# A hybrid layer whose weights come packed by quarters, and half of x transposed: x's second half scaled by VectorE alone, and other steps for heads and gate rows

## The chip, the cores and the metric

The kernel runs on one core of one Trainium2 chip. The metric is device microseconds from start to end of one execution, median over runs. The kernel before took 1518.96 us (three runs: 1516.54, 1518.96, 1522.65).

## What is computed

One layer of a hybrid encoder for one sequence of 1024 tokens of width 2048, all in float32:

```
h = RMSNorm(x) * norm_w
proj = h @ w_in                      # 2048 -> 6656 columns: rq rk rv rg | aq ak av ag
y_ret = groupnorm(retention(rq, rk, rv)) * silu(rg)      # 8 heads x 128, both directions, chunks of 128
y_att = window_attention(aq, ak, av, sink) * silu(ag)    # 8 heads, 2 kv heads, window of 128
out = RMSNorm(x + concat(y_ret, y_att) @ w_out) * final_norm_w
```

The two projections hold nearly all of the arithmetic.

## The kernel before

**Products.** A float32 matrix is split into a high and a low part of a matmul type. `mm3` multiplies high by high, high by low and low by high, so a product of two tiles is three matmuls (lines 99, 100 and 101). The high part is a cast by ScalarE (`wH`, line 88), the low part a subtraction by VectorE (`wL`, line 85).

**Blocks, products, steps.** The input projection is done in blocks of 512 columns by half of the 2048 rows of `w_in`, 26 of them in four phases. A block is not four quarter products but seven products of sums and differences (numbers 1, 2, 6, 5, 7, 3, 4). The sums on the weights' side are made while the kernel runs from the block's four quarters `a11`, `a12`, `a21`, `a22` (loaded by `quarter`) and a temporary `s2`; those of x's side (`c1` to `c7`) are made once for each half of x's columns. A product is four steps of two PSUM banks by three matmuls, so 24 matmuls of 128x512; a block is 28 steps. `pj` are the banks: two (`X`) for products 1, 6, 7 and 4, two (`Y`) for 2, 5 and 3. `evict` takes a finished bank away into a tile `ct`: ScalarE copies after products 1, 6, 5 and 4, VectorE adds after the others.

**What sets the order.** TensorE, SyncE (which issues most DMAs) and GpSimd run in the order in which the program is written; for VectorE and ScalarE a scheduler picks the order at build time, except in a few pinned places. At run time every engine works its own list strictly in order. `advance()` stands after every step of a product; it is the kernel's clock. All other work (turning x, rotary, the heads, attention, gates) is written as jobs, generators that are advanced once a step, so a `yield` in a job moves what follows by one step, and `idle(n)` by n. `prepare()` makes one product's operand a product ahead, in two buffers each of `wH` and `wL`, so a cast waits until the product two before has been multiplied.

**x.** x's first 1024 columns are transposed by TensorE at the start. Its second 1024 columns come in `second_part()` (line 489) while the blocks of the first phase run: 16 loads `xp` of 256 KB, 16 scalings by the row's `rms` on VectorE (line 500), 64 transposes on TensorE (line 463, in groups of four) and 16 copies by ScalarE that multiply by `norm_w` (line 464). The tile `src` that comes out feeds the sums for phases 2 and 4 (additions are line 92, subtractions line 95). `scale_first()` spreads `rms` along a row for the first half (`factors`, `rows`) and scales with it.

**Heads.** `head(h)` (line 824) runs eight times, one after the other: decays, scores (line 841), `vd`, v scaled by ScalarE (line 855, four operations), outer products of k and `vd` (line 870), states, results.

**Gates and the seam.** In the last phase `gating()` (line 1298) starts. `gate()` loads eight gate rows and eight rows of mixed heads, one pair after another, and `mix_in()` multiplies them into `ysrc` (line 1328). `puts()` makes the operand sums for the output projection from `ysrc` while the last block still runs, and the projection starts as they come. Its weights come as half quarters (line 1218).

Of the kernel before, what the change touches and what calls it, by code (L numbers as in the profile page):

```python
# [9 lines left out]
F32 = mybir.dt.float32  # L10
# [8 lines left out]
P = 128  # L19
# [19 lines left out]
M = 4  # L39
# [19 lines left out]
def hybrid_layer_kernel(  # L59
    ctx: ExitStack,  # L60
    tc: tile.TileContext,
    x, w_in, w_out, norm_w, decay_fwd, decay_bwd, gn_w, gn_b, sink, final_norm_w,
    rot_r, rot_a, dist_f, dist_b, steps, band,
    out,
):
    nc = tc.nc
    x, w_in, w_out, out = x[0], w_in[0], w_out[0], out[0]

# [39 lines left out]
    def blk(i, n=1):  # L108
        return slice(i * P, (i + n) * P)
# [19 lines left out]
    def idle(n):  # L129
        for _ in range(n):  # L130
            yield
# [49 lines left out]
    wp = ctx.enter_context(tc.tile_pool(name="wp", bufs=1))  # L181
    w_v = w_in.rearrange("(k p) c -> p k c", p=P)

# [11 lines left out]
    def quarter(part, b, n, k):  # L195
        t = wp.tile([P, M, 2 * P], F32, name=f"a{n}{k}", tag=f"a{n}{k}")
        k0, c0 = (2 * part + k - 1) * M, BLOCKS[b] + 2 * P * (n - 1)
        nc.sync.dma_start(out=t, in_=w_v[:, k0:k0 + M, c0:c0 + 2 * P])
        return t
# [259 lines left out]
    def turn(dst, parts, k):  # L459

        pt = ax()
        for i, part in enumerate(parts):
            nc.tensor.transpose(pt[:, blk(i)], part, ident)
        nc.scalar.activation(out=dst, in_=pt, func=AF.Copy, scale=nw[:, k:k + 1])
# [24 lines left out]
    def second_part():  # L489
        x2 = x[:, PART:].rearrange("s (h c) -> s h c", h=2)  # L490
        src = None
        for j in range(2):
            for m in range(2):
                xp = []
                for t in range(4 * m, 4 * m + 4):
                    xp.append(st.tile([P, 2, 2 * P], F32, name="xp", bufs=4))
                    nc.sync.dma_start(out=xp[-1], in_=x2[blk(t), :, 2 * P * j:2 * P * (j + 1)])
                yield from idle(10)
                for i in range(4):
                    nc.vector.tensor_scalar(out=xp[i], in0=xp[i], scalar1=rms[:, 4 * m + i:4 * m + i + 1], scalar2=None, op0=ALU.mult)  # L500
                yield from idle(3)
                if src is None:
                    src = st.tile([P, 2, M, S], F32, name="src", tag="src")
                for s in range(2):
                    for i in range(2):
                        turn(src[:, s, 2 * j + i, half(m)], [xp[t][:, s, blk(i)] for t in range(4)], (2 + s) * M + 2 * j + i)
                        yield
        parts_of(1, src)
        for sums, _ in parts[1]:
            yield from idle(4)  # L510
            sums()
# [6 lines left out]
    def half_of_a11(k0):  # L518
        c0 = BLOCKS[units[0][1]]
        nc.sync.dma_start(out=a11[:, k0:k0 + 2], in_=w_v[:, k0:k0 + 2, c0:c0 + 2 * P])  # L520

# [236 lines left out]
    def retention():  # L758
        with right("ret") as ret:
# [64 lines left out]
            def head(h):  # L824
# [7 lines left out]
                while h and turned.get(h - 1) != 2:  # L832
                    yield
                yield
                kT, qT = kq.pop(("kT", h)), kq.pop(("qT", h))
# [17 lines left out]
                for d in range(2):  # L853
                    for m in range(2):
                        nc.scalar.mul(vd[:, m * M:m * M + M, d].rearrange("p c (a j) -> p c a j", a=NB), v[m], kd[:, d * RH + h:d * RH + h + 1])
                    yield
                while h not in ks:
                    yield
# [204 lines left out]

    def scale_first():

        yield
        yield
        factors, rows = (st.tile([P, HALF], F32, name=n, tag="xp", bufs=4) for n in ("factors", "rows"))
        rows_of.append(rows)
        nc.vector.tensor_copy(out=chunks(factors), in_=rms[:, 0:4].rearrange("p (t o) -> p t o", o=1).broadcast_to([P, 4, P]))  # L1070
# [4 lines left out]
        nc.scalar.copy(out=rows, in_=pt)  # L1075
        yield

# [117 lines left out]
    free = set()  # L1195
    wo_v = w_out.rearrange("(k p) c -> p k c", p=P)
    wo_ = ctx.enter_context(ExitStack())
# [32 lines left out]
    def out_operands():  # L1230

        at = dict(PLACES)
        for u in range(len(OUT)):
# [16 lines left out]
            if u == len(OUT) - 1:  # L1250
                again = combp.tile([P, 2, 2, HALF], F32, name="again", tag="c1")
                part, pair = OUT[u]
                for j in range(2):
                    nc.sync.dma_start(out=again[:, j], in_=wo_v[:, M + 2 * j:M + 2 * j + 2, half(2 * pair + 1)])
                for j in range(2):
# [42 lines left out]
    def gating():  # L1298
# [13 lines left out]
        def operand_tiles(part, gates):  # L1312
# [18 lines left out]
            def gate():  # L1331
                asked = 0
                for i in range(2 * M):
# [229 lines left out]

_INS = ["x", "w_in", "w_out", "norm_w", "decay_fwd", "decay_bwd", "gn_w", "gn_b", "sink", "final_norm_w"]
_OUTS = [((1, S, D), "float32")]
# [24 lines left out]
```

## Time and profile before

| what | before |
|---|---|
| median of three runs | 1518.96 us |
| the profiled execution | 1518.94 us, its span 1517.2 us |
| TensorE busy | 1493.9 us, 98% |
| VectorE, ScalarE, GpSimd busy | 1111.8 us, 687.7 us, 150.0 us |
| moved by DMA | 318.91 MB, mean 210 GB/s |
| DMA packets under 2 KB | 110882 of 189704 |

Matmuls are pipelined: a 128x512 matmul is listed with some 0.39 us, but the next starts 0.23 us after it, so TensorE's pace is read from the starts. A window row of the profile gives for a stretch the busy time of each engine with its count of instructions, the clock that TensorE was granted (1.00 is full) and the DMA engines' busy share and GB/s. A wait row names the instruction that stood, what it waited for, the time in all, how often, and the longest.

### The profile page before, as it was taken

How to read it: one execution, taken by the hardware profiler on the slowest of the kernel's cores; microseconds unless marked ns; L12 is line 12 of the kernel's file. 1: busy time of each engine (PE TensorE's matmuls, PEld its weight loads, DVE VectorE, ACT ScalarE, POOL GpSimd, SP SyncE). 2: the span in 40 equal slices, each digit the busy share in tenths (PEclk: the TensorE clock that was granted, in tenths of full speed). 3: DMA queues.
4: the chain of work that ended last, by engine and by line, in shares of the span. 5: the costliest groups of instructions: out<-in, count | busy, mean ns of one | idle time of the engine just before them, and what ended most of it. 6: DMA issues, size and time to landing. Idle time of an engine off the chain costs nothing.

```text
span 1517.2 us, 20252 instructions
## 1 busy us (share of the span) xinstructions
PE 1493.9 (98%) x7214; PEld 1256.4 (83%) x7214; DVE 1111.8 (73%) x1935; ACT 687.7 (45%) x1123; POOL 150.0 (10%) x177
## 2 busy tenths in 40 slices
PE   9999999999999999999999999999999999999997
PEld 7888888788888888888888888887888788888886
DVE  6896594657758585867988989887656946776766
ACT  6553462234535453533534544444444563542425
POOL 0000001121010000001211100000211102020001
PEclk9999999999999999999999999999999999999999
DMA  8279847889675527798867765499896889495656
GB/s 319 70 269 327 312 167 182 221 212 253 160 221 194 199 93 224 266 332 188 164 178 177 190 201 168 146 318 318 216 262 163 185 194 209 88 209 171 212 179 252
DMA packets 189704, 318.91 MB, mean 210 GB/s; under 512 B 31618, under 2 KB 110882, under 8 KB 180771
## 3 DMA queue, kind: packets, MB, share of 16 engines
q1 hardware_dynamic: 165554, 266.74, 53.7%
q0 software_dynamic: 19728, 36.71, 16.3%
q10 hardware_dynamic: 4320, 14.17, 2.7%
q8 instruction: 57, 0.93, 0.3%
q14 instruction: 45, 0.36, 0.1%
HBM read 197.23 MB, written 128.71 MB: 215 GB/s over the span
## 4 chain that ended last, share of the span: by engine, by line
PE 72%; issue 10%; DVE 8%; DMA 6%; ACT 1%; SPq 1%; POOL 1%; ACTq 0%; POOLq 0%; DVEq 0%
PE pj L101 18%; PE pj L100 18%; PE pj L99 18%; PE ax L100 5%; PE ax L101 4%; PE ax L99 4%; DMA pr<-ct 2%; DVE wL L85 2%; PE ax L870 2%; DMA xt<-in_x_dram 1%; PE ax L653 1%; DVE ct L92 1%; DMA q<-pr 1%; PE ax L841 1%; PE ax L921 1%
## 5 line engine op out<-in xcount | busy, mean ns | idle before, releaser
L99 PE MATMUL pj<-c,wH 128*128 128x512 f32 x1444 | 574.3, 398 | 0.1
L101 PE MATMUL pj<-c,wL 128*128 128x512 f32 x1440 | 563.3, 391 | 2.3 <-DVE wL L85 2.2
L100 PE MATMUL pj<-c,wH 128*128 128x512 f32 x1444 | 563.6, 390 | 0.0
L101 PEld LDWEIGHTS pj<-c,wL 128*128 128x128 f32 x1440 | 270.7, 188 | 61.7 <-DVE wL L85 4.4
L99 PEld LDWEIGHTS pj<-c,wH 128*128 128x128 f32 x1444 | 271.7, 188 | 51.2 <-ACT wH L88 0.5
L100 PEld LDWEIGHTS pj<-c,wH 128*128 128x128 f32 x1444 | 272.0, 188 | 50.8 <-DVE c L999 0.2
L85 DVE TENSOR_TENSOR wL<-a,wH 128x1024 fp32r<-128x1024 f32 x157 | 191.5, 1220 | 116.6 <-ACT wH L88 109.6
L88 ACT CAST wH<-a 128x1024 fp32r<-128x1024 f32 (+1 forms) x159 | 166.2, 1045 | 227.2 <-PE pj L100 138.6
L325 ACT COPY ct<-pj 128x512 f32<-128x512 f32 x192 | 110.7, 584 | 183.6 <-PE pj L101 182.5
L92 DVE TENSOR_TENSOR ct<-pj,ct 128x512 f32<-128x512 f32 x164 | 109.3, 686 | 53.6 <-PE pj L101 50.1
L289 POOL DMA_DIRECT2D pr<-ct x88 | 78.0, 958 | 543.9 <-DVE ct L92 466.2
L85 DVE TENSOR_TENSOR wL<-s,wH 128x1024 fp32r<-128x1024 f32 x56 | 68.3, 1220 | 54.0 <-ACT wH L88 47.0
L100 PE MATMUL pj<-wL,c 128*128 128x512 f32 x224 | 88.2, 394 | 2.7 <-DVE wL L85 2.7
L99 PE MATMUL pj<-wH,c 128*128 128x512 f32 x224 | 87.8, 392 | 0.0
L101 PE MATMUL pj<-wH,c 128*128 128x512 f32 x224 | 87.8, 392 | 0.0
L100 PE MATMUL ax<-wL,c 128*128 128x512 f32 x208 | 81.2, 390 | 0.1
L101 PE MATMUL ax<-wH,c 128*128 128x512 f32 x208 | 81.0, 389 | 0.0
L99 PE MATMUL ax<-wH,c 128*128 128x512 f32 x208 | 81.0, 389 | 0.0
L88 ACT CAST wH<-s 128x1024 fp32r<-128x1024 f32 x56 | 58.9, 1052 | 37.8 <-DVE s L95 12.8
L100 PEld LDWEIGHTS pj<-wL,c 128*128 128x128 f32 x224 | 42.4, 189 | 12.2 <-DVE wL L85 3.6
L643 ACT ACTIVATE s<-s,nm 128x385 f32<-128x385 f32 (+1 forms) x64 | 37.6, 589 | 28.5 <-DVE nm L638 25.8
L947 ACT ACTIVATE y<-y,mv,rstd 128x128 f32<-128x128 f32 x64 | 26.9, 485 | 51.2 <-DVE mv L945 51.1
(242 smaller groups left out, 2053.2 us busy)
## 6 DMA issues: line engine op xcount, KB each, us to landing
a<-in_w_in_dram SPq DMA_DIRECT2D x103, 512.0 KB, 6.1
kept<-c SPq DMA_DIRECT2D x28, 1024.0 KB, 7.3
c<-kept SPq DMA_DIRECT2D x28, 1024.0 KB, 9.4
pr<-ct SPq DMA_DIRECT2D x94, 256.0 KB, 4.8
pr<-ct POOLq DMA_DIRECT2D x88, 256.0 KB, 6.0
a<-in_w_out_dram SPq DMA_DIRECT2D x18, 512.0 KB, 5.2
rx<-pr SPq DMA_DIRECT2D x64, 128.0 KB, 5.8
ysrc<-pr ACTq DMA_DIRECT2D x16, 512.0 KB, 5.1
```

The lines of the kernel that those rows point to most:

```text
L85: return nc.vector.tensor_tensor(out=dst, in0=src, in1=high.bitcast(F32), op=ALU.subtract)
L88: behind(pinned, nc.scalar.copy(out=dst_h, in_=src))
L92: nc.vector.tensor_tensor(out=dst, in0=a, in1=b, op=ALU.add)
L99: nc.tensor.matmul(po, aH, bH, start=first, stop=False, **kw)
L100: nc.tensor.matmul(po, aH, bL, start=False, stop=False, **kw)
L101: nc.tensor.matmul(po, aL, bH, start=False, stop=last, **kw)
L289: nc.gpsimd.dma_start(out=dst, in_=t, accum_op=ALU.add)
L325: nc.scalar.copy(out=t, in_=bank)
L643: nc.scalar.activation(out=s[:, 0:w + 1], in_=s[:, 0:w + 1], func=AF.Exp, scale=-1.0, bias=nm, accum_out=den)
L653: nc.tensor.transpose(pt[:, blk(j)], s[:, blk(j)], ident)
L870: nc.tensor.matmul(p, k_tok[:, c // 2, :, c % 2], vd[:, c, d], start=True, stop=True)
L947: nc.scalar.activation(out=y[:, c], in_=y[:, c], func=AF.Identity, scale=rs[:, c:c + 1], bias=mv[:, c, 0:1])
```

## The change

Three things are changed together.

1. `w_in` is given packed: each quarter of a block (128 partitions x 4 x 256) is one contiguous piece of 512 KB, so that a partition's part is 4 KB in one run where it was four runs of 1 KB. `w_out` is packed likewise, 4 KB in one run where it was two of 2 KB.
2. x's second 1024 columns are given transposed as `x_t`, in addition to x. `second_part()` now waits for step 66, loads four pieces of 1 MB at steps 66, 69, 72 and 75 straight into `src`, spreads `rms` of the second 512 tokens along rows (one VectorE copy, four transposes, one ScalarE copy) and scales `src` with eight operations of 128x1024 on VectorE, one a step from step 85. `factors` and `rows` get tiles of their own.
3. A head's scores come after two steps where it was one, its outer products after one more step. The waits between gate rows of the first part are 5 steps for the first four rows and 4 for the others, where all were 6.

By the program's own count of steps, the second part is ready at step 92 where it was 117. Heads' scores move from steps 435, 464, 488, 516, 540, 568, 592, 620 to 436, 465, 491, 518, 544, 571, 597, 624. The gating job starts at 651 where it was 646, but asks for its first row at 656 in both. Its eighth row of the first part is mixed at 710 where it was 718, and the sums of the output projection's products 2 and 6 are made at 713 and 717 where it was 718 and 720.

```diff
     def quarter(part, b, n, k):
         t = wp.tile([P, M, 2 * P], F32, name=f"a{n}{k}", tag=f"a{n}{k}")
         k0, c0 = (2 * part + k - 1) * M, BLOCKS[b] + 2 * P * (n - 1)
-        nc.sync.dma_start(out=t, in_=w_v[:, k0:k0 + M, c0:c0 + 2 * P])
+        nc.sync.dma_start(out=t, in_=w_in[k0 // M, c0 // (2 * P)])
         return t
...
     def second_part():
-        x2 = x[:, PART:].rearrange("s (h c) -> s h c", h=2)
-        src = None
-        for j in range(2):
-            for m in range(2):
-                xp = []
-                for t in range(4 * m, 4 * m + 4):
-                    xp.append(st.tile([P, 2, 2 * P], F32, name="xp", bufs=4))
-                    nc.sync.dma_start(out=xp[-1], in_=x2[blk(t), :, 2 * P * j:2 * P * (j + 1)])
-                yield from idle(10)
-                for i in range(4):
-                    nc.vector.tensor_scalar(out=xp[i], in0=xp[i], scalar1=rms[:, 4 * m + i:4 * m + i + 1], scalar2=None, op0=ALU.mult)
+        yield from idle(66 - clock[0])
+        src = st.tile([P, 2, M, S], F32, name="src", tag="src")
+        for s in range(2):
+            for j in range(2):
+                nc.sync.dma_start(out=src[:, s, 2 * j:2 * j + 2], in_=x_t[s][:, 2 * j:2 * j + 2])
                 yield from idle(3)
-                if src is None:
-                    src = st.tile([P, 2, M, S], F32, name="src", tag="src")
-                for s in range(2):
-                    for i in range(2):
-                        turn(src[:, s, 2 * j + i, half(m)], [xp[t][:, s, blk(i)] for t in range(4)], (2 + s) * M + 2 * j + i)
-                        yield
+        rows = rows_of[1]
+        yield from rows_from(rms[:, 4:8], rows[:, half(1)])
+        yield from idle(4)
+        for s in range(2):
+            for k in range(M):
+                i = (2 + s) * M + k
+                nc.vector.scalar_tensor_tensor(out=src[:, s, k], in0=src[:, s, k], scalar=nw[:, i:i + 1], in1=rows, op0=ALU.mult, op1=ALU.mult)
+                yield
         parts_of(1, src)
...
                 while h and turned.get(h - 1) != 2:
                     yield
-                yield
+                yield from idle(2)
                 kT, qT = kq.pop(("kT", h)), kq.pop(("qT", h))
...
                     for m in range(2):
                         nc.scalar.mul(vd[:, m * M:m * M + M, d].rearrange("p c (a j) -> p c a j", a=NB), v[m], kd[:, d * RH + h:d * RH + h + 1])
                     yield
+                yield
                 while h not in ks:
...
-        nc.sync.dma_start(out=t, in_=wo_v[:, k0:k0 + 2, half(2 * pair + n - 1)])
+        nc.sync.dma_start(out=t, in_=w_out[k0 // 2, 2 * pair + n - 1])
...
-                    yield from idle(6 if part == 0 else 5)
+                    yield from idle(5 if part == 0 and i < M else 4 if part == 0 else 5)
```

**VectorE, the block that runs when x's second half is scaled.** In these rows `wL<-a` and `wL<-s` are low parts of operands, `ct` are evictions, and a number behind a name is that of a buffer. Before:

```order
L1098 TENSOR_TENSOR ct<-ct 128x512 x2
L500 TENSOR_SCALAR xp<-xp,rms 128x512
L92 TENSOR_TENSOR ct<-pj,ct 128x512 x2
L85 TENSOR_TENSOR wL<-a_773,wH 128x1024
L500 TENSOR_SCALAR xp<-xp,rms 128x512 x3
L85 TENSOR_TENSOR wL<-a_816,wH 128x1024
L85 TENSOR_TENSOR wL<-s_984,wH 128x1024
L92 TENSOR_TENSOR ct<-pj,ct 128x512 x2
L85 TENSOR_TENSOR wL<-a_901,wH 128x1024
```

Changed, at the later place where the eight long operations stand (line 504):

```order
L85 TENSOR_TENSOR wL<-a_893,wH 128x1024
L504 SCALAR_TENSOR_TENSOR src<-src,vec_t,rows 128x1024 x3
L92 TENSOR_TENSOR ct<-pj,ct 128x512 x2
L85 TENSOR_TENSOR wL<-a_1089,wH 128x1024
L504 SCALAR_TENSOR_TENSOR src<-src,vec_t,rows 128x1024 x4
L85 TENSOR_TENSOR wL<-a_1091,wH 128x1024
L95 TENSOR_TENSOR a_1089<-a_1089,a_1051 128x1024
L504 SCALAR_TENSOR_TENSOR src<-src,vec_t,rows 128x1024
L95 TENSOR_TENSOR s_1254<-a_1170,a_1089 128x1024
L1103 TENSOR_TENSOR ct<-ct 128x512 x2
L85 TENSOR_TENSOR wL<-s_1254,wH 128x1024
```

The short scalings that were spread over two blocks are gone; eight long ones now stand between the low parts of three products, in groups of three, four and one.

**ScalarE, the start of the block in which the last head has its outer products.** Here `pj_9177` and `pj_9178` (before) and `pj_9038` and `pj_9039` (changed) are the two banks of product 4 of the block ahead, `pj_9652` and `pj_9653` (before) and `pj_9521` and `pj_9522` (changed) those of this block's product 1. `wH<-s2` is the operand of product 6, the third. Before:

```order
L325 COPY ct_9638<-pj_9177 128x512
L88 CAST wH_9656<-a12_9375 128x1024
L325 COPY ct_9643<-pj_9178 128x512
L88 CAST wH_9716<-s2_9660 128x1024
L855 ACTIVATE vd_9685<-v_tok_9562,kd_213 128x4x128 x4
L325 COPY ct_9701<-pj_9652 128x512
L325 COPY ct_9706<-pj_9653 128x512
L88 CAST sH_9708<-st_9731 128x2x128
```

Changed:

```order
L327 COPY ct_9505<-pj_9038 128x512
L88 CAST wH_9525<-a12_9218 128x1024
L88 CAST wH_9571<-s2_9529 128x1024
L327 COPY ct_9510<-pj_9039 128x512
L327 COPY ct_9558<-pj_9521 128x512
L853 ACTIVATE vd_9596<-v_tok_9464,kd_213 128x4x128 x2
L327 COPY ct_9563<-pj_9522 128x512
L853 ACTIVATE vd_9596<-v_tok_9464,kd_213 128x4x128 x2
L88 CAST wH_9617<-a21_9155 128x1024
```

The last head's `vd` still stands behind the same cast, now with copies ahead of and between its parts, and the copy of the second bank of product 4 has come behind that cast, where it stood ahead of it. The bank that it frees is taken next by the second bank of `Y` in this block, which product 2 uses first.

**VectorE, the end of the last block, where gated rows are mixed (line 1328, now 1332) and the output projection's sums follow.** Before:

```order
L1328 TENSOR_TENSOR ysrc<-ysrc,yt 128x1024
L92 TENSOR_TENSOR ct<-pj,ct 128x512 x2
L85 TENSOR_TENSOR wL<-a_10453,wH 128x1024
L85 TENSOR_TENSOR wL<-a_10455,wH 128x1024
L95 TENSOR_TENSOR a_10453<-a_10453,a_10414 128x1024
L95 TENSOR_TENSOR s_10598<-a_10523,a_10453 128x1024
L92 TENSOR_TENSOR a_10414<-a_10414,a_10523 128x1024
L1328 TENSOR_TENSOR ysrc<-ysrc,yt 128x1024
L85 TENSOR_TENSOR wL<-s_10598,wH 128x1024
```

Changed:

```order
L1332 TENSOR_TENSOR ysrc<-ysrc,yt 128x1024
L92 TENSOR_TENSOR ct<-pj,ct 128x512
L85 TENSOR_TENSOR wL<-a_10135,wH 128x1024
L1332 TENSOR_TENSOR ysrc<-ysrc,yt 128x1024
L92 TENSOR_TENSOR ct<-pj,ct 128x512 x2
L85 TENSOR_TENSOR wL<-a_10329,wH 128x1024
L85 TENSOR_TENSOR wL<-a_10331,wH 128x1024
L95 TENSOR_TENSOR a_10329<-a_10329,a_10288 128x1024
L95 TENSOR_TENSOR s_10477<-a_10402,a_10329 128x1024
L92 TENSOR_TENSOR a_10288<-a_10288,a_10402 128x1024
L85 TENSOR_TENSOR wL<-s_10477,wH 128x1024
```

One mixing of 128x1024 that stood ahead of the low part of `s` now stands ahead of that block's first low parts.

More of the change, by code (lines that the diff above doesn't have):

```diff
@@ L61, in hybrid_layer_kernel @@
     tc: tile.TileContext,
-    x, w_in, w_out, norm_w, decay_fwd, decay_bwd, gn_w, gn_b, sink, final_norm_w,
+    x, x_t, w_in, w_out, norm_w, decay_fwd, decay_bwd, gn_w, gn_b, sink, final_norm_w,
     rot_r, rot_a, dist_f, dist_b, steps, band,
@@ L66, in hybrid_layer_kernel @@
     nc = tc.nc
-    x, w_in, w_out, out = x[0], w_in[0], w_out[0], out[0]
+    x, out = x[0], out[0]
     const = ctx.enter_context(tc.tile_pool(name="const", bufs=1))
@@ L181, in hybrid_layer_kernel, with w_at @@
     wp = ctx.enter_context(tc.tile_pool(name="wp", bufs=1))
-    w_v = w_in.rearrange("(k p) c -> p k c", p=P)
+    def w_at(k0, c0):
+        return w_in[k0 // M, c0 // (2 * P)]
     def comb_tile(i):
@@ L197, in quarter @@
         k0, c0 = (2 * part + k - 1) * M, BLOCKS[b] + 2 * P * (n - 1)
-        nc.sync.dma_start(out=t, in_=w_v[:, k0:k0 + M, c0:c0 + 2 * P])
+        nc.sync.dma_start(out=t, in_=w_at(k0, c0))
         return t
@@ L519, in half_of_a11 @@
         c0 = BLOCKS[units[0][1]]
-        nc.sync.dma_start(out=a11[:, k0:k0 + 2], in_=w_v[:, k0:k0 + 2, c0:c0 + 2 * P])
+        nc.sync.dma_start(out=a11[:, k0:k0 + 2], in_=w_at(0, c0)[:, k0:k0 + 2])
     load_first(nc.sync, 0, 0)
@@ L1062, in sums_of_x, with rows_from @@
                     start(scale_first())
[L1064 to L1070, printed above, removed]
+    def rows_from(of, rows):
+        factors = st.tile([P, HALF], F32, name="factors")
+        nc.vector.tensor_copy(out=chunks(factors), in_=of.rearrange("p (t o) -> p t o", o=1).broadcast_to([P, 4, P]))
         yield from idle(3)
@@ L1075, in scale_first @@
         nc.scalar.copy(out=rows, in_=pt)
+    def scale_first():
+        yield
+        yield
+        both = st.tile([P, S], F32, name="rows")
+        rows = both[:, half(0)]
+        rows_of.extend((rows, both))
+        yield from rows_from(rms[:, 0:4], rows)
         yield
@@ L1195, in hybrid_layer_kernel @@
     free = set()
-    wo_v = w_out.rearrange("(k p) c -> p k c", p=P)
     wo_ = ctx.enter_context(ExitStack())
@@ L1253, in out_operands @@
                 for j in range(2):
-                    nc.sync.dma_start(out=again[:, j], in_=wo_v[:, M + 2 * j:M + 2 * j + 2, half(2 * pair + 1)])
+                    nc.sync.dma_start(out=again[:, j], in_=w_out[M // 2 + j, 2 * pair + 1])
                 for j in range(2):
@@ L1561, in _tables, with _laid_out @@
     }
-_INS = ["x", "w_in", "w_out", "norm_w", "decay_fwd", "decay_bwd", "gn_w", "gn_b", "sink", "final_norm_w"]
+def _laid_out(np, inputs):
+    x, w_in, w_out = (np.asarray(inputs[n])[0] for n in ("x", "w_in", "w_out"))
+    return {
+        "x_t": x.T.reshape(4, M, P, S).transpose(0, 2, 1, 3)[2:],
+        "w_in": w_in.reshape(4, M, P, -1, 2 * P).transpose(0, 3, 2, 1, 4),
+        "w_out": w_out.reshape(KT // 2, 2, P, -1, HALF).transpose(0, 3, 2, 1, 4),
+    }
+_INS = ["x", "x_t", "w_in", "w_out", "norm_w", "decay_fwd", "decay_bwd", "gn_w", "gn_b", "sink", "final_norm_w"]
 _OUTS = [((1, S, D), "float32")]
@@ L1576 @@
     arrays, args = {}, []
-    given = {n: inputs[n] for n in _INS}
+    given = {n: inputs.get(n) for n in _INS}
     given.update(_tables())
+    given.update(_laid_out(_np, inputs))
     for name, v in given.items():
```

## The prediction

> **What bounds the kernel now.** I read the page's first part, then the waits of TensorE, then windows of the places where these waits stand.
>
> ```profile
> span 1517.2 us, 20252 instructions
> ...
> PE 1493.9 (98%) x7214; PEld 1256.4 (83%) x7214; DVE 1111.8 (73%) x1935; ACT 687.7 (45%) x1123; POOL 150.0 (10%) x177
> ```
>
> TensorE is busy for 98% of the span. So only two things can make this kernel shorter: fewer instructions on TensorE, or fewer of its waits. These are the longest waits by instruction (total, times, longest):
>
> ```profile
> PE ax L870 <- ACT vd L855: 2.9, 2, 1.6
> PE pj L100 <- DVE wL L85: 2.7, 2, 2.5
> PE pj L101 <- DVE wL L85: 2.2, 3, 0.9
> PE ax L841 <- DVE qT L92: 1.8, 2, 1.2
> ```
>
> The first two stand at two places: the last head's outer products, and the seam at which the output projection takes over. Windows of both (us, PE, PEld, DVE, ACT, POOL busy, clock, DMA share, GB/s):
>
> ```profile
> 1036.00:1042.00 6.00, 3.09 (x17) 2.28 (x16) 4.11 (x4) 4.41 (x7) 0.00 (x0) 1.00 1.01 317
> 1042.00:1046.00 4.00, 4.00 (x17) 3.42 (x16) 1.81 (x6) 0.86 (x3) 0.00 (x0) 0.58 1.05 384
> 1208.00:1212.00 4.00, 1.53 (x7) 0.97 (x6) 4.00 (x4) 3.01 (x4) 0.00 (x0) 1.00 1.22 187
> 1212.00:1216.00 4.00, 4.00 (x13) 3.09 (x12) 3.77 (x4) 1.06 (x1) 0.00 (x0) 0.58 0.92 213
> ```
>
> At both, TensorE is idle for 2.9 us (6.00 - 3.09) and 2.5 us (4.00 - 1.53), and the 4 us behind are granted a clock of 0.58 only. A stretch of 4 us at 0.58 loses 4 x 0.42 = 1.7 us, so each of these waits costs more than its length.
>
> [...]
>
> **The change, part by part.**
>
> *Transposes.* TensorE loses 64 transposes and gains 4, so 15 groups of four go.
>
> ```profile
> 104.26 0.40 PE L101 MATMUL pj<-c,wL 128*128 128x512 f32 x1
> 104.50 0.60 PE L463 MATMUL ax<-ident,xp 128*128 128x128 f32 x4
> 104.85 0.48 PE L99 MATMUL pj<-c,wH 128*128 128x512 f32 x1
> 105.17 0.39 PE L100 MATMUL pj<-c,wH 128*128 128x512 f32 x1
> 105.40 0.40 PE L101 MATMUL pj<-c,wL 128*128 128x512 f32 x1
> ```
>
> ```profile
> L463 PE MATMUL ax<-ident,xp 128*128 128x128 f32 x64 | 9.6, 272 | 0.0
> ```
>
> From the matmul at 104.26 to the second one behind it, at 105.17, pass 0.91 us with a group of four between; two plain steps are 2 x 0.23 = 0.46 (105.17 to 105.40). A group costs 0.45 us, 15 of them 6.8 us: **-6.8**. The ends are -6.5 (rounding of the starts) and -9.0 (60 of 64 by the group's busy time of 9.6). No wait stands with them (0.0 in the last column), so all of it is on the path.
>
> *VectorE's eight scalings.* The trace has no such operation at 128x1024. The nearest rows:
>
> ```profile
> L1446 DVE SCALAR_TENSOR_TENSOR ra<-r,rs,fw 128x512 f32<-128x512 f32 x8 | 6.0, 746 | 2.4 <-POOL rs L1427 2.4
> ...
> L1079 DVE TENSOR_TENSOR src<-src,rows 128x512 f32<-128x512 f32 x8 | 5.0, 687 | 0.0
> ...
> L95 DVE TENSOR_TENSOR tt<-src 128x1024 f32<-128x1024 f32 x4 | 4.9, 1220 | 1.7 <-ACT src L464 1.7
> ```
>
> Twice the elements add 1220 - 687 = 533 ns to a tensor by tensor; 746 + 533 makes 1.28 us, between 1.22 (a plain one) and 1.49 (twice 746). Eight are 10.2 us, on an engine with room elsewhere, but they stand close together. In the order of the changed kernel four stand between the low part for one product and that for the next. A product lasts 24 x 0.23 = 5.5 us. Its low part can come late by what is left after the cast (1.0) and itself (1.2), 3.3 us. Four scalings take 5.1, so the next low part is up to 1.8 us late if VectorE had nothing done ahead, and 0 if it had. I take the middle, **+1.0**. The far end: four at 1.49 are 6.0, less 3.3 makes 2.7, and if that also costs the clock, 4.4.
>
> *The loads of x_t.* The bytes are the same (4 MB), but they come in one third of the time, where the queues are already full:
>
> ```profile
> 102.00:118.00 16.00, 16.00 (x80) 13.26 (x79) 13.61 (x18) 6.13 (x9) 0.00 (x0) 1.00 0.85 294
> 118.00:130.00 12.00, 12.00 (x59) 9.97 (x58) 3.36 (x4) 4.93 (x8) 0.00 (x0) 1.00 0.91 312
> 130.00:142.00 12.00, 12.00 (x59) 9.93 (x58) 10.02 (x13) 4.22 (x7) 0.00 (x0) 1.00 0.92 309
> ```
>
> ```profile
> 120.50 0.94 SPq L198 DMA_DIRECT2D a<-in_w_in_dram  x2
> ```
>
> ```profile
> a<-in_w_in_dram SPq DMA_DIRECT2D x103, 512.0 KB, 6.1
> ...
> ysrc<-pr ACTq DMA_DIRECT2D x16, 512.0 KB, 5.1
> ...
> xt<-in_x_dram SPq DMA_DIRECT2D x7, 1024.0 KB, 9.2
> ```
>
> The last piece is asked for at step 75, behind the pair of weight quarters on SyncE's queue at 120.50, so at about 122 us; a load of 1 MB took 9.2 us: 131. Scalings begin at step 85, about 133 us, and the last piece is first used six steps on, at 141. If 3 MB more go through at 312 GB/s ahead of it, everything slides by 9.6 us, to 141. I take **0**: the cover is these 10 us. If they are gone, VectorE stands at the last two scalings with the next low parts queued behind them (the last rival).
>
> *Packing.* A quarter of `w_in` landed after 6.1 us, 512 KB in longer runs (`ysrc`) after 5.1. None of the long waits above is for a weight quarter, so 1 us earlier is hidden behind the products that run ahead of it. At the start, where the first quarters and x come together, some of it may show: between 0 and two quarters' 1.0, so 2.0; I take **-0.5**. [...]
>
> *Heads.* Two heads' scores waited for `qT`, 1.8 us in all, longest 1.2. With one more step (6 x 0.23 = 1.4 us) in between, both are over: **-1.8** (lower end 0, if `qT` only comes later). The step moves with it the next head's loads on SyncE; the last head is late by four steps, 5.4 us, and no row of the gates waits for it, since their first row is asked at step 656 in both.
>
> The last head:
>
> ```profile
> 1037.59 1.04 ACT L88 CAST wH<-s 128x1024 fp32r<-128x1024 f32 x1 [5.75 <-PE pj L100]
> 1038.55 2.56 ACT L855 ACTIVATE vd<-v_tok,kd 128x512 f32<-128x512 f32 x4
> 1041.01 1.04 ACT L325 COPY ct<-pj 128x512 f32<-128x512 f32 x2
> ```
>
> ```profile
> 1037.35 0.39 PE L101 MATMUL pj<-c,wL 128*128 128x512 f32 x1
> 1039.32 0.50 PE L870 MATMUL ax<-vd,k_tok 128*128 128x128 f32 x2 [1.58 <-ACT vd L855]
> ```
>
> ScalarE stood for 5.75 us before a cast that TensorE had to release, and `vd`, which needs nothing of that, stood behind it. TensorE came for it at 1037.7, step 624. In the changed order `vd` is still behind that cast, and three `ct` copies as well: ready at 1038.55 + 2.56 + 3 x 0.52 = 1042.7. But TensorE now comes at step 629, 5 x 1.4 later, at 1044.5. So the wait goes, with its slow stretch: 2.9 + 1.7 = **-4.6** (nearest the row, as 1.8 us of room remain; lower end 0).
>
> What is late next is in the same rows of the order: the copy of the second bank of product 4 now stands behind this cast. That bank is taken by product 2, which starts when product 1's end releases the cast. Cast and copy end 1.04 + 0.52 later; TensorE needs the bank after three matmuls, 0.68. So a new wait of **+0.9** (0 if the bank is needed later; 1.6 if at once).
>
> *The seam.* VectorE is full from 1160 on, so the seam's 2.5 us are what it has too much:
>
> ```profile
> 1150.00:1160.00 10.00, 10.00 (x46) 8.29 (x45) 4.69 (x5) 2.08 (x3) 2.78 (x5) 1.00 1.04 202
> 1170.00:1180.00 10.00, 10.00 (x46) 8.29 (x45) 10.00 (x10) 4.97 (x6) 1.78 (x2) 1.00 0.51 107
> ```
>
> ```profile
> 1164.08 1.22 DVE L92 TENSOR_TENSOR a<-a,a 128x1024 f32<-128x1024 f32 x1
> 1165.21 1.22 DVE L1328 TENSOR_TENSOR ysrc<-ysrc,yt 128x1024 f32<-128x1024 f32 x1
> ```
>
> The change takes one mixing (1.13 us from start to start) out of the full part and into 1150 to 1160, which is half empty. The wait of 2.5 becomes 1.4. That is about half of either wait that has a slow stretch behind it, so I also take the stretch out: 1.1 + 1.7 = **-2.8**, ends -1.1 (the clock falls all the same) and -4.2 (all of it goes).
>
> *Sum.* -6.8 + 1.0 + 0 - 0.5 - 1.8 - 4.6 + 0.9 - 2.8 = -14.6 us. The profiled execution took 1518.94, its span and 1.7 us around it; the median of the runs is 1518.96, so no correction: **1504.3 us**.
>
> **The rivals.**
>
> *Only the transposes are gained.* New positions move every job by some steps, and waits that go here come back there: 1.8, 4.6 and 2.8 are 9.2 us in four places. If two thirds of them return, the time is 1510.4, if all return with the +0.9 and +1.0 it is 1513.5. For it: the schedule has only two places with a wait over 2 us among some hundred operands, and any new order may make one, as that of the copy above does. Against: the order shows no other such place.
>
> *VectorE becomes the bound where x is scaled.* +4.4 in place of +1.0 gives 1507.7. For it: four long scalings in a row; against: 3.36 of 12 us busy in the window ahead.
>
> *More goes than I count.* The seam's wait gone as a whole (-4.2), no waits at the scalings and the copy (-1.9), transposes at -9.0: 1498.8.
>
> *The slow clock does not follow the waits.* Then both stretches at 0.58 stay, 2 x 1.7: 1507.7. [...] The rows speak against it: both stretches stand directly behind a wait.
>
> *Slower: x_t lands late.* VectorE works strictly in its order; the last two scalings wait for the last piece, the low parts of the next products behind them, and TensorE stands. It costs nothing up to 141 + 3.3 us, then its full length. To end at 1526.5 it would have to land 22 us later still, at 166, 44 us after it was asked for, against 9.2 for such a load.
>
> **How the numbers follow.** Forecast, with its own range of 1499.5 to 1507: 0.52. VectorE or the clock, near 1507.7 (up to 1509): 0.15. Only the transposes, 1509 to 1515: 0.17, half of it on each side of 1511.4. More than counted, below 1499.5: 0.10. Between 1515 and 1526.5: 0.03; slower: 0.03. The range from 1496 to 1512 leaves out about 0.15. 0.5% is about what a measurement of this kernel tells from no change, so faster is below 1511.4 and slower above 1526.5: 0.52 + 0.15 + 0.10 + 0.08 = 0.85 faster, 0.12 same, 0.03 slower.
>
> **What would show it.** In the changed profile: a line of 4 transposes for `factors` where there were 64 for `xp`, and TensorE's busy time less by about 7 us; the scalings near 1.28 us each, and whether a wait of `L101` or `L100` for `wL` stands at 135 to 165 us; no wait of the outer products for `vd`, none of the scores for `qT`; one wait of some 0.9 us for a copy `ct` at the last head; at the seam a wait of about 1.4 us and a clock of 1.00 behind it. The forecast is wrong if low parts are late by several us at the scalings, if a new wait of over 2 us with a slow stretch stands anywhere, or if the seam is as it was.

## The result, and the profile after

The changed kernel takes 1513.1 us (median of six runs, 1510.18 to 1514.02) against 1520.01 (six runs of the kernel before beside it, 1516.54 to 1522.65): a ratio of 0.9953, 95% interval 0.9939 to 0.9968. That is 7 us less where 14.6 were forecast, and 1.1 us above the wide range of 1496 to 1512. The profiled execution took 1510.18 us, the fastest of the six.

Its page, first part:

```profile
span 1508.1 us, 20087 instructions
...
PE 1484.3 (98%) x7154; PEld 1248.6 (83%) x7154; DVE 1115.7 (74%) x1928; ACT 678.8 (45%) x1108; POOL 150.3 (10%) x177
```

TensorE has the 60 instructions fewer (7214 to 7154), and it is still busy for 98%. All waits of TensorE in the changed kernel (total, times, longest):

```profile
PE pj L99 <- ACT ct L327: 5.9, 3, 2.9
PE pj L101 <- DVE wL L85: 3.9, 6, 1.0
PE pj L100 <- DVE wL L85: 1.9, 1, 1.9
PE pj L1142 <- POOL ident masks.py:199: 1.4, 1, 1.4
PE ax L839 <- PE pj L101: 0.8, 1, 0.8
PE ax L465 <- DVE xt L459: 0.5, 1, 0.5
PE pj L365 <- ACT c L994: 0.2, 1, 0.2
```

The rest of the list of the kernel before, whose first four rows the prediction shows:

```profile
PE pj L1137 <- POOL ident masks.py:199: 1.4, 1, 1.4
PE ax L1013 <- DMA xt<-in_x_dram: 1.2, 1, 1.2
PE ax L463 <- DVE xt L457: 0.9, 1, 0.9
PE pj L363 <- ACT c L995: 0.2, 1, 0.2
PE ax L653 <- DVE s L641: 0.2, 1, 0.2
```

The waits for `vd`, for the `qT` of two earlier heads and for x's first transfer are gone. In their place stands a kind that the kernel before did not have: `L99` waits three times, 5.9 us, for a copy `ct`, so for a PSUM bank to be emptied. Added up, the lists hold 13.5 us before and 14.6 after. The change has not taken waits out; it has exchanged them. The 0.8 us of the scores (`L839`) is listed for a matmul, but looks like a wait for `qT` again, now at the last head: the matmul before it started 1.2 us earlier, and VectorE's last operation on this `qT` ended (1030.04 + 0.68) 0.11 us before the scores began:

```profile
1029.63 0.39 PE L101 MATMUL pj<-c,wL 128*128 128x512 f32 x1
1030.83 1.13 PE L839 MATMUL ax<-qT,kT 128*128 128x128 f32 x8 [0.81 <-PE pj L101]
```

```profile
1030.04 0.68 DVE L92 TENSOR_TENSOR qT<-qT,rx 128x512 f32<-128x512 f32 x1
```

The slow stretches are the other half. Windows of the changed kernel at the last head and at the seam (columns as in the prediction):

```profile
1032.00:1036.00 4.00, 1.15 (x5) 0.64 (x4) 3.95 (x5) 2.08 (x4) 0.00 (x0) 1.00 1.25 248
1036.00:1040.00 4.00, 4.00 (x24) 3.43 (x23) 2.77 (x4) 2.88 (x5) 0.00 (x0) 1.00 0.94 356
1204.00:1208.00 4.00, 3.26 (x14) 2.70 (x15) 4.00 (x4) 1.51 (x3) 0.00 (x0) 1.00 1.00 196
```

TensorE was busy for 1.15 of 4 us, and yet the clock behind it is 1.00, where the kernel before had two stretches at 0.58 (a mean over 4 us; the last run below shows it in windows of 1 us). The profiled execution adds up: 6.8 us of transposes, 1.1 us more waits, 3.4 us of slow clock less make 9.1, and the spans differ by 9.1 (1517.2 to 1508.1). The median gained 2 us less than that. The last run below shows why.

### The profile page after: what moved, and what is told of

Read it like the earlier page. It is cut to its first block, busy times and chain, and to the rows that moved or that the text cites. A ratio compares the mean times of both kernels' runs of the same rounds, so it can differ in the third digit from the quotient of the medians.

```text
span 1508.1 us, 20087 instructions
## 1 busy us (share of the span) xinstructions
PE 1484.3 (98%) x7154; PEld 1248.6 (83%) x7154; DVE 1115.7 (74%) x1928; ACT 678.8 (45%) x1108; POOL 150.3 (10%) x177
## 4 chain that ended last, share of the span: by engine, by line
PE 81%; DMA 3%; DVE 2%; issue 1%; ACT 0%; SPq 0%; POOL 0%; ACTq 0%; POOLq 0%; DVEq 0%
PE pj L101 21%; PE pj L99 21%; PE pj L100 21%; PE ax L100 5%; PE ax L101 5%; PE ax L99 5%; PE ax L869 2%; PE ax L651 1%; PE ax L920 1%; PE ax L839 1%; DVE wL L85 1%; DMA c<-kept 1%; DMA g<-mix 1%; DMA pr<-ct 0%; DMA ysrc<-pr 0%
## 5 line engine op out<-in xcount | busy, mean ns | idle before, releaser
L99 PE MATMUL pj<-c,wH 128*128 128x512 f32 x1444 | 572.7, 397 | 5.9 <-ACT ct L327 5.9
L101 PE MATMUL pj<-c,wL 128*128 128x512 f32 x1440 | 562.8, 391 | 3.9 <-DVE wL L85 3.9
L101 PEld LDWEIGHTS pj<-c,wL 128*128 128x128 f32 x1440 | 270.4, 188 | 64.1 <-DVE wL L85 7.1
L99 PEld LDWEIGHTS pj<-c,wH 128*128 128x128 f32 x1444 | 271.5, 188 | 58.5 <-ACT ct L327 7.2
L99 PE MATMUL pj<-wH,c 128*128 128x512 f32 x224 | 87.2, 389 | 0.0
L101 PE MATMUL pj<-wH,c 128*128 128x512 f32 x224 | 87.2, 389 | 0.0
L101 PE MATMUL ax<-wH,c 128*128 128x512 f32 x208 | 81.0, 389 | 0.0
L99 PE MATMUL ax<-wH,c 128*128 128x512 f32 x208 | 80.9, 389 | 0.0
L99 PEld LDWEIGHTS pj<-wH,c 128*128 128x128 f32 x224 | 42.1, 188 | 8.8
L101 PEld LDWEIGHTS pj<-wH,c 128*128 128x128 f32 x224 | 42.1, 188 | 8.6
```

Source lines behind the costliest of these rows:

```text
L99: nc.tensor.matmul(po, aH, bH, start=first, stop=False, **kw)
L101: nc.tensor.matmul(po, aL, bH, start=False, stop=last, **kw)
```

## The experiments

Times are given as ratios to the kernel before, run beside each on the same chip, with the 95% interval; a tenth of a per cent is 1.5 us. Where only one place of the program is at stake, the wait there is read in the trace.

### Each part alone

**The x part.** Weights unpacked, steps of heads and gate rows as before:

```diff
-        return w_in[k0 // M, c0 // (2 * P)]
+        return w_v[:, k0:k0 + M, c0:c0 + 2 * P]
-                yield from idle(2)
+                yield
-                    yield from idle(5 if part == 0 and i < M else 4 if part == 0 else 5)
+                    yield from idle(6 if part == 0 else 5)
```

> Only the second part of the change is made (x_t, 60 transposes fewer, eight scalings on VectorE); weights unpacked, heads and gate rows step as before. Theory 'copies' (in the changed kernel TensorE's new waits are for PSUM banks whose copies stand behind a waiting cast on ScalarE): its order has the same copies behind the cast while x is scaled, so the two waits of 1.7 and 1.4 us stand at 143 to 163 us, and the time is 6.8 - 3.3 = 3.5 us less than before, ratio 0.998. Rival 'elsewhere' (the scaling is harmless, the lost time belongs to heads and gates): 6 to 7 us less, ratio 0.9955.

Measured: 0.9961 (0.9949 to 0.9972), 5.9 us less, 1513.57. Its longest waits where x is scaled:

```profile
145.62 0.50 PE L99 MATMUL pj<-c,wH 128*128 128x512 f32 x1 [1.65 <-ACT ct L329]
162.99 0.50 PE L99 MATMUL pj<-c,wH 128*128 128x512 f32 x1 [1.44 <-ACT ct L329]
```

Both waits came, as theory 'copies' said, and yet 3.5 us (0.9977) lies just outside the interval and the rival's 0.9955 inside. In the profiled execution the waits add up to 15.7 us where 13.5 were, so 6.8 - 2.2 = 4.6 us were to be expected and the span is 5.8 shorter; 1.2 us of that are in no list, nor in the clock, for both profiles have a slow stretch at the last head and at the seam (0.58 and 0.58 before; 0.89 and 0.68, and 0.73 and 0.85 here, where each falls on two windows of 4 us; 1.7 us by either). What is sure is that this part holds most of what the whole change gained. At the last head, whose steps are as before here, TensorE is listed as waiting 2.21 us for the DMA that brings `k_tok`, and 0.73 for `vd`; with the packing alone it is 2.28 and 0.66, with the gate rows alone 3.03 for `k_tok`. So `vd` was one of two late inputs there, and not the only one.

**The packing.** Only the layout of `w_in` and `w_out`.

> Only the packing of w_in and w_out is made. The prediction's term: -0.5 us, ratio 0.9997. Rival: packing hastens DMAs all over (packets under 2 KB fall from 110882 to some 53000) and takes 2 us or more out of waits: ratio below 0.9987. [...]

Measured: 0.9994 (0.9985 to 1.0004). The median landing of a `w_in` quarter goes from 6.1 to 6.0 us, although packets under 2 KB fall from 110882 to 57633:

```profile
DMA packets 144775, 318.91 MB, mean 210 GB/s; under 512 B 31617, under 2 KB 57633, under 8 KB 135842
...
a<-in_w_in_dram SPq DMA_DIRECT2D x103, 512.0 KB, 6.0
```

The forecast of half a microsecond lies in the interval, and so does nothing.

**The heads' steps.**

```diff
                while h and turned.get(h - 1) != 2:
                    yield
-                yield
+                yield from idle(2)
...
+                yield
                 while h not in ks:
```

> Only the heads' extra steps are made. Theory 'copies': its order again has one bank copy behind the cast of s2 in the last head's block, so the 4.6 us of that place turn into a wait of about 3 us for a copy, and with the scores' waits (1.8) gone: 3 us less, ratio 0.998. The prediction's sizes (4.6 + 1.8 - 0.9): 5.5 us less, ratio 0.9964.

Measured: 0.9997 (0.9989 to 1.0006). Less than both. At the last head:

```profile
1034.98 1.13 PE L845 MATMUL ax<-qT,kT 128*128 128x128 f32 x8 [0.82 <-PE pj L101]
...
1039.67 0.51 PE L99 MATMUL pj<-c,wH 128*128 128x512 f32 x1 [2.85 <-ACT ct L329]
```

The waits for `vd` and `qT` went, and 3.7 us at the same head came; low parts that are late at other heads took much of the rest (3.7 us in five waits of `L101`, where 2.2 in three were). All waits add up to 12.7 us where 13.5 were, and a slow stretch stands behind the new wait too (0.57 from 1040 to 1044), so neither the 4.6 us nor the 1.8 came.

**The gate rows' steps.**

```diff
-                    yield from idle(6 if part == 0 else 5)
+                    yield from idle(5 if part == 0 and i < M else 4 if part == 0 else 5)
```

> Only the steps between gate rows are made. The prediction's term for the seam: -2.8 us, with the slow stretch of 1.7 gone; ratio 0.998. Rival: the slow stretch at the seam does not follow from the length of the wait, and stays: -0.5 to -1.1, ratio 0.9995.

Measured: 0.9995 (0.9982 to 1.0007). The wait at the seam shrinks from 2.47 to 1.93 us, half of what moving 1.13 us of VectorE's work was to give. The row of VectorE shows where most of the other half went: the low part of `s`, which stood behind the moved mixing before, now waits 0.70 us for its cast. And the slow stretch is still there:

```profile
1166.68 1.23 DVE L85 TENSOR_TENSOR wL<-s,wH 128x1024 fp32r<-128x1024 f32 x1 [0.70 <-ACT wH L88]
```

```profile
1211.41 0.50 PE L100 MATMUL pj<-wL,c 128*128 128x512 f32 x1 [1.93 <-DVE wL L85]
```

```profile
1212.00:1216.00 4.00, 4.00 (x12) 3.15 (x11) 3.90 (x4) 2.11 (x2) 0.00 (x0) 0.57 1.07 198
```

The time agrees with the rival; the prediction's term, a ratio of 0.998, lies at the edge of the interval. In the profile of the whole change the wait is as long (1.92) and has no slow stretch. Over all profiles of this study the shorter wait does matter: behind a seam of 2.47 us the stretch stands in four of four (the kernel before and the three runs above), behind one of 1.92 or 1.93 in five of thirteen.

### Why a bank is emptied late

ScalarE, VectorE and TensorE of the changed kernel at the last head:

```profile
1033.92 1.04 ACT L88 CAST wH<-s 128x1024 fp32r<-128x1024 f32 x1 [6.80 <-DVE s L95]
1034.88 1.07 ACT L327 COPY ct<-pj 128x512 f32<-128x512 f32 x2
```

```profile
1031.36 0.69 DVE L92 TENSOR_TENSOR qT<-qT,rx 128x512 f32<-128x512 f32 x1
1031.99 0.69 DVE L842 TENSOR_TENSOR sd<-ax,dT 128x512 f32<-128x512 f32 x1
1032.60 1.21 DVE L95 TENSOR_TENSOR s<-a,a 128x1024 f32<-128x1024 f32 x1
```

```profile
1035.51 0.50 PE L99 MATMUL pj<-c,wH 128*128 128x512 f32 x1 [2.85 <-ACT ct L327]
```

The copy was ready to run when ScalarE came to the cast of `s2`; the cast stood for 6.8 us, and not for a product's end, as the prediction had it, but for VectorE's sum `s`, which stood behind the rotation of q and the scores. Product 1's last matmul started at 1029.63; the sum ended at 1033.81, about 4 us later, and the cast began 0.11 us after it. Two causes are possible: the copy's place behind the cast, or VectorE's lateness, which would show in `wL` if the copy came first.

**All casts and copies held in program order at the last head** (steps 616 to 628):

```diff
-        split(wH[:, k0:k1], wL[:, k0:k1], src[:, k0:k1])
+        behind(616 <= clock[0] <= 628, nc.scalar.copy(out=wH[:, k0:k1], in_=src[:, k0:k1]))
+        low(wL[:, k0:k1], src[:, k0:k1], wH[:, k0:k1])
...
-            nc.scalar.copy(out=t, in_=bank)
+            behind(616 <= clock[0] <= 628, nc.scalar.copy(out=t, in_=bank))
```

> The changed kernel with ScalarE's casts of operands and copies of banks held in program order from step 616 to 628, so that both copies of product 4 come ahead of the cast of s2. Theory 'copies': the wait of 2.9 us for the copy at the last head goes, and the 0.8 of the scores there may too: 3 to 4 us less than the changed kernel, 1509 to 1510. Rival 'VectorE late': the cast of s2 and its low part are late because VectorE makes them late, so TensorE only waits a product later, for wL: the same time as the changed kernel.

Measured: 0.9963 (0.9948 to 0.9977), no different from the changed kernel. The copy's wait is gone, and two others are there:

```profile
1032.92 0.50 PE L101 MATMUL pj<-c,wL 128*128 128x512 f32 x1 [2.04 <-DVE wL L85]
...
1041.08 0.50 PE L101 MATMUL pj<-c,wL 128*128 128x512 f32 x1 [1.52 <-DVE wL L85]
```

**The same where x is scaled**, with low parts and scalings held in order too (steps 80 to 112):

> The changed kernel with casts, bank copies, low parts and the eight scalings held in program order from step 80 to 112; the bank copies come ahead of the casts there, but VectorE's order is then four scalings, a sum, two evictions and two scalings between two low parts. Theory 'copies': the two waits of 1.7 and 1.4 us go: 3 us less than the changed kernel. Rival 'VectorE late': they turn into waits for wL at 140 to 165 us of the same size: no change.

Measured: 1.0014 (1.0004 to 1.0025): worse than expected by either, 9 us behind the changed kernel. The two copies' waits went, and VectorE was late for 6.29 us in one wait; all waits add up to 21.2 us, and slow stretches at this place cost 5.1 more (sum of 4 us windows):

```profile
171.39 0.80 PE L101 MATMUL pj<-c,wL 128*128 128x512 f32 x1 [6.29 <-DVE wL L85]
```

Both edits also made the scheduler reorder VectorE, so they do not separate the causes. One thing can be read from the first: there VectorE has finished `qT` by 1027.32, and the scores' 0.81 is gone.

**Half of the scaling's work.** The scalings take `half(0)` of the tokens alone, so the second 512 tokens of x's second half stay unscaled.

> The changed kernel with the eight scalings over half of the rows only (the second 512 tokens of x's second half are left unscaled), so 5 us less work for VectorE there; ScalarE's order is the same. Theory 'copies': the second wait (1.4 us, behind a cast that waits for the end of a product) stays, and the first shrinks to about the same, since the cast then waits for the product too: at most 0.5 us gained. Rival 'VectorE late': both waits go, 3 us less than the changed kernel.

Measured: 0.9957 (0.9943 to 0.9972), the same as the changed kernel. The first wait shrinks from 1.66 to 0.76, the second stays (1.44 to 1.39):

```profile
144.63 0.50 PE L99 MATMUL pj<-c,wH 128*128 128x512 f32 x1 [0.76 <-ACT ct L327]
...
161.96 0.50 PE L99 MATMUL pj<-c,wH 128*128 128x512 f32 x1 [1.39 <-ACT ct L327]
```

So VectorE's scalings have no part in the second, whose cast waits for a product's end; in the first, VectorE's lateness is about half.

**Both places held in program order, scalings two steps apart.**

> Both places held in program order, and the scalings two steps apart, so that the copies are ahead of the casts and VectorE has fewer scalings between two low parts. Theory 'copies': 6 us less than the changed kernel, 1507. Rival 'VectorE late': 0 to 3 us less.

Measured: 0.9976 (0.9966 to 0.9986). No wait for a copy is left, and one of 4.1 us for `wL` where x is scaled: again the reordered VectorE.

**Scaling early.** Rows first, and each piece scaled when it should have landed:

```diff
+        def scales():
+            yield from rows_from(rms[:, 4:8], rows[:, half(1)])
+            for n, at in enumerate((74, 77, 81, 86)):
+                yield from idle(at - clock[0])
+                ...
```

> The changed kernel with the rows made ready first and each piece of x_t scaled as soon as it should have landed (steps 74, 77, 81 and 86, two scalings each) instead of all eight from step 85. ScalarE's order of casts and copies is the same. Theory 'VectorE late' (the waits at 143 and 161 us come from VectorE being full there): the first wait (1.8 us) goes nearly whole, the second (1.6), behind a cast that waits for a product's end only, stays: 1 to 2 us less than the changed kernel, 1511.5. Theory 'copies' alone: no change. Rival: a piece has not landed when its scaling stands first in VectorE's order, low parts wait behind it, and 2 us or more are lost.

Measured: 0.9958 (0.9944 to 0.9971). The first wait goes from 1.66 to 1.29 only:

```profile
145.39 0.50 PE L99 MATMUL pj<-c,wH 128*128 128x512 f32 x1 [1.29 <-ACT ct L327]
...
162.72 0.50 PE L99 MATMUL pj<-c,wH 128*128 128x512 f32 x1 [1.40 <-ACT ct L327]
```

At the second place about 1.4 us is the price of a copy behind a cast that a product's end releases: cast and copy, 1.04 and 0.52, for a bank that is wanted at once. At the first the cast is still held by VectorE's sum, so the 1.29 is not that price alone:

```profile
143.62 1.05 ACT L88 CAST wH<-s 128x1024 fp32r<-128x1024 f32 x1 [4.30 <-DVE s L95]
```

**The last rotation late.**

```diff
-                    yield from idle(2)
+                    yield from idle(6 if (name, h) == ("qT", RH - 1) else 2)
```

> The changed kernel with the last head's q loaded and rotated four steps later, which puts VectorE's sum for s2 ahead of the rotation. Theory 'VectorE late': the cast of s2 then waits for the product's end only, so the wait of 3.0 us for the copy shrinks to some 1.5, and the scores' 1.0 goes: 2.5 us less than the changed kernel, 1510.5. Rival: the last head's other work is only moved and the same waits stand four steps later: no change.

Measured: 0.9958 (0.9946 to 0.9971), 1511.55. The wait shrinks from 2.85 to 1.78, the scores' 0.81 is gone, and a second one for a copy, 1.06, is new:

```profile
1032.21 0.50 PE L99 MATMUL pj<-c,wH 128*128 128x512 f32 x1 [1.78 <-ACT ct L327]
...
1039.97 0.50 PE L99 MATMUL pj<-c,wH 128*128 128x512 f32 x1 [1.06 <-ACT ct L327]
```

That is 0.8 us of waits less, not 2.5, and nothing that the ratio shows. The sum now ends at 1030.52, 3.3 us earlier, but it is still what the cast waits for (3.76 us), not the product's end.

**Both of these.**

> Both of these: if both theories hold, 4 us less than the changed kernel, 1509, and the fastest kernel of the study.

Measured: 0.9952 (0.994 to 0.9965), 1510.68: by the ratio no faster than the changed kernel. The 4 us expected did not come; both places kept waits for a copy (1.29 and 1.39, 1.79 and 1.06).

**Only the casts of `s2` and the copies after products 4 and 6 held in order at the last head**, which leaves VectorE as it was but for one low part:

```diff
-        split(wH[:, k0:k1], wL[:, k0:k1], src[:, k0:k1])
+        behind(s and (612 <= clock[0] <= 630), nc.scalar.copy(out=wH[:, k0:k1], in_=src[:, k0:k1]))
+        low(wL[:, k0:k1], src[:, k0:k1], wH[:, k0:k1])
...
-            yield operand(s2)
+            yield operand(s2, s=True)
...
-            nc.scalar.copy(out=t, in_=bank)
+            behind(i in (4, 6) and (612 <= clock[0] <= 630), nc.scalar.copy(out=t, in_=bank))
```

> The changed kernel with only the casts of s2 and the copies after products 4 and 6 held in program order from step 612 to 630. On ScalarE one cast moves behind three copies and two parts of vd; on VectorE only the low part of that operand moves, behind the second scores' scaling. Theory 'copies' (TensorE stands for a bank whose copy is queued behind a cast that waits): the wait of 3.0 us at the last head goes, the scores' 1.0 stays; at most 1 us comes back at wL: 2 to 3 us off the span of the changed kernel with the same clock, 1510 to 1511. Theory 'VectorE late': the 3.0 come back as waits for wL, as when all casts were held: no change.

Measured: 0.9948 (0.9936 to 0.9961), 1510.52. ScalarE now takes the copy of product 4's second bank at 1026.83, before the cast of `s2`, and the 2.85 are gone; 1.52 come back at `wL`. By the ratio this is 0.7 us better than the changed kernel, which the intervals do not resolve. ScalarE, VectorE, and TensorE's new wait:

```profile
1026.83 0.58 ACT L327 COPY ct<-pj 128x512 f32<-128x512 f32 x1
...
1033.71 1.05 ACT L194 CAST wH<-s 128x1024 fp32r<-128x1024 f32 x1 [2.26 <-DVE s L95]
```

```profile
1037.56 1.37 DVE L92 TENSOR_TENSOR ct<-pj,ct 128x512 f32<-128x512 f32 x2 [1.39 <-PE pj L101]
1038.85 1.22 DVE L85 TENSOR_TENSOR wL<-s,wH 128x1024 fp32r<-128x1024 f32 x1
```

```profile
1040.12 0.50 PE L101 MATMUL pj<-c,wL 128*128 128x512 f32 x1 [1.52 <-DVE wL L85]
```

The cast had ended at 1034.76. The low part starts 4 us later because the edit put it on VectorE behind two evictions that wait for TensorE. So the 1.52 come from the edit's order, and not from `s` being late.

**The same where x is scaled.**

> The same from step 86 to 112, where x is scaled; VectorE keeps its eight scalings in place. Theory 'copies': the waits of 1.8 and 1.6 us go, 3 us less than the changed kernel: 1510. Theory 'VectorE late': wL waits of the same size.

Measured: 0.9956 (0.9944 to 0.9969), 1511.68. Both copies' waits are gone; waits of 0.55, 0.97 and 0.53 stand in their place, so 2.1 of 3.1 us come back. At the second place the cast of `s2` now stands behind a copy that starts at 164.75, and begins at 165.24, where it began at 161.40 in the changed kernel: the 0.97 and 0.53 there are again of the edit's making.

So both theories hold in part. A copy behind a waiting cast makes TensorE wait for the bank, and with the copy ahead that wait goes. VectorE's lateness adds to it where the cast waits for a sum: at the last head (2.85, and 1.78 with the sum earlier) and at the first place where x is scaled (1.66, and 0.76 with half of the scaling). The half to two thirds that came back in the last two runs do not show how late VectorE is, since holding the order had also put the operand's cast or low part behind other work.

**All of it.** Copies ahead at both places, scaling early, rotation late:

> Copies ahead of casts at both places, the scalings early and the last rotation late: by theory 'copies' 6 us less than the changed kernel, 1507, the fastest of the study; by theory 'VectorE late', where this relief came already with the run of both, 1510.7.

Measured: 0.9938 (0.9924 to 0.9951), 1510.23: the fastest of the study, some 2 us below the changed kernel, though the two intervals overlap. By the ratio a third of the 6 us came. At the last head a wait of 2.55 for `wL` is left, with a slow stretch behind it (0.65 from 1040 to 1044): this time sum and cast are early, and the low part stands on VectorE behind the rotation and the scores. At the first place where x is scaled a wait of 1.33 for a copy is left, although the copies now stand ahead of the cast:

```profile
144.50 1.56 ACT L327 COPY ct<-pj 128x512 f32<-128x512 f32 x3 [5.47 <-issue]
145.94 1.07 ACT L194 CAST wH<-s 128x1024 fp32r<-128x1024 f32 x1
```

The first copy starts 0.08 us after VectorE's pair of operations on `ct` tiles (line 1110) ends at 144.42. All `ct` share eight buffers, so it may have waited for one of these; no run isolates that. If it did, that is a third way for a bank to be emptied late.

### The same kernel once more

> The changed kernel once more, profiled anew. Theory 'clock by chance': the same waits stand at the same places, but a slow stretch of TensorE's clock stands behind one or both of those at 1032 and 1202 us, where the first profile had none, and the span is 1.7 to 3.4 us longer. Rival: the executions differ in their waits, not in the clock.

Measured: 1513.32 us, span 1511.4, 3.3 us more than in the first profile.

```profile
1032.00:1036.00 4.00, 1.77 (x11) 1.29 (x11) 3.96 (x5) 0.96 (x2) 0.00 (x0) 1.00 1.20 295
1036.00:1040.00 4.00, 3.37 (x12) 3.09 (x13) 3.15 (x5) 4.00 (x8) 0.00 (x0) 0.59 0.97 324
```

The same wait (2.86 for the copy) now has a slow stretch behind it. In windows of 1 us:

```profile
1036.00:1037.00 1.00, 0.37 (x1) 0.38 (x2) 0.95 (x2) 1.00 (x4) 0.00 (x0) 0.84 1.12 197
1037.00:1038.00 1.00, 1.00 (x3) 0.76 (x3) 0.96 (x2) 1.00 (x3) 0.00 (x0) 0.50 0.97 377
1038.00:1039.00 1.00, 1.00 (x6) 0.95 (x5) 1.00 (x2) 1.00 (x3) 0.00 (x0) 0.50 0.96 403
1039.00:1040.00 1.00, 1.00 (x6) 1.00 (x6) 0.24 (x2) 1.00 (x2) 0.00 (x0) 0.50 0.81 318
```

So the clock is 0.50, and what it takes adds up to 0.16 + 3 x 0.50 + 0.05 (the next window shows 0.95) = 1.7 us, which makes 1.7 / 0.50 = 3.4 us at that clock; the 0.57 to 0.59 of the wider windows are means. The waits add up to 15.4 us where the first profile had 14.6. Both are 2.5 of the 3.3 us; the rest is not in the wait list.

So whether a wait costs the clock too differs between two executions of one kernel, and the profile of the fastest execution showed neither stretch. It is not mere chance, though. Over the 17 profiles the stretch stands behind none of 23 single waits of 1.29 to 1.79 us, six of 15 of 1.92 to 2.04, and 13 of 15 of 2.21 to 3.03; three times it stands behind two shorter ones close together (1.58 and 1.33 before, 0.96 and 1.18 with the scalings in order, 1.56 in all with half of them). Behind the copy's 2.85 at the last head it stands in six of seven profiles, behind the 1.92 at the seam in five of thirteen: 1.7 x (6/7 + 5/13) = 2.1 us in a usual execution, an estimate from these counts. With the waits of the kernel before it is three of four and four of four, 3.0 us. So the clock gave about 0.9 us in the usual execution and not the 3.4 of the first profile: 6.8 - 1.1 + 0.9 = 6.6 us, near the 7 of the medians.

## Why the prediction was wrong

- **Transposes, -6.8: right.** 60 instructions fewer, and the sum of the profiled execution closes with it; that it closes to 0.1 us is luck, since the same sum is off by 1.2 us for the x part and by 0.8 for the second profile.
- **Scalings, +1.0: mis-sized, and by another way.** One takes 1278 ns, as estimated (1.28):

```profile
L504 DVE SCALAR_TENSOR_TENSOR src<-src,vec_t,rows 128x1024 f32<-128x1024 f32 x8 | 9.8, 1278 | 0.0
```

  No low part was late there. The cost was two waits of 1.7 and 1.4 us for banks. The step that failed: only VectorE's order was read at this place, not ScalarE's, which has the same copy behind the cast as the last head. At the first of the two places about half is VectorE after all, through the sum that the cast waits for.
- **Loads of x_t, 0: right.** They landed 8.4 us (median) after their issue, the last of them issued at 119 us, and no scaling waited (0.0 in the row above).
- **Packing, -0.5: not told from 0.** The term counted on a quarter of `w_in` landing 1.0 us earlier (5.1 us, as `ysrc`, for 6.1). It landed after 6.0 us with the packing alone and after 5.8 in the changed kernel, and the ratio of the packing alone, 0.9994, has 1 in its interval.
- **Scores, -1.8: the two waits went**, but most of it came back: 0.8 us at the last head's scores, and 1.5 us more of late low parts, at other heads. The heads' steps alone gained nothing (0.9997).
- **Last head, -4.6 + 0.9: the step that failed by most.** The wait for `vd` went as worked out (`k_tok` was late there too, which the prediction did not see), and the new wait for the bank was at the place named. Its size was 2.85 with 0.8 at the scores, not 0.9. The prediction took the cast to be released by product 1's end; it was held by its own input, the sum `s` on VectorE, until some 4 us after product 1's last matmul had started. And the new wait is as long as the one that went, so the slow stretch came back with it in six of seven profiles. In place of -3.7 this head gave about nothing, by these lists and counts.
- **Seam, -2.8: the wait shrank by 0.5, not 1.1**, since VectorE then stood 0.70 us for a cast that the moved mixing had covered. The slow stretch was counted as removed for certain; it went in eight of thirteen profiles. That makes about 0.5 + 1.7 x 8/13 = 1.6 us, an estimate.
- **The sum.** Waits and clock were to give 7.8 us besides the transposes. By the median they gave about nothing; the interval of the ratio leaves 4.9 to 9.3 us for everything together. The rival "only the transposes are gained" (1510.4 to 1513.5) was what happened, by the way that it named: waits that go come back elsewhere. Of the four parts run alone only the x part differs from no change by more than its interval.
- **The clock.** The fourth rival, that the slow clock does not follow the waits, does not hold: in the windows of 4 us of all 17 profiles (0 to 368, 500 to 864 and 1000 to 1356 us) every slow stretch stands behind waits. But the length of a wait alone does not settle it: 1.92 or 1.93 us at the seam was followed by a slow stretch in five profiles of thirteen, and 2.85 at the last head was followed by none in one of seven. What sets a stretch off is not shown by any run.

## What to carry to other kernels

Before a wait is counted as gone, look in every engine's order at what stands behind an instruction that waits, above all copies that free a buffer behind a cast for later work: there the blocked engine passes its wait to the one that needs the buffer (here 6.80 us before a cast on ScalarE became 2.85 us on TensorE). For each such instruction take the latest of all its inputs, not only the one that is plain. Putting the copy ahead helps only if the same edit does not put the cast or the low part behind other work that waits. Count what certainly leaves the bound engine in full, and waits that are only moved at about nothing until the order shows that nothing late stands behind them. A slow stretch behind a wait is counted with its chance, read from several profiles, and not as certain from one (here six of seven at the last head, five of thirteen at the seam).

## What was not expected of the hardware

A wait of 1.9 to 3 us was followed by a clock of 0.50 for about 3.4 us (in windows of 1 us in the second profile of the changed kernel) in some executions, and by a clock of 1.00 in others: behind the copy's wait at the last head 1.00 in the first profile of that kernel and 0.59 over 4 us in the second. Each stretch takes 1.7 us, on two places, so up to 3.4 us of a run's time. No single wait of up to 1.79 us was followed by one; of those from 2.21 to 3.03 us 13 of 15 were. Runs of the changed kernel lay between 1510.18 and 1514.02.
